# Down and output projections of a two-layer encoder trunk: activations stationary, weights streamed 512 columns at a time, sums turned back by TensorE

## The chip, the cores and the metric

The kernel runs on one NeuronCore of a Trainium2 chip. The metric is the device time of one execution in microseconds (us); the figure of a kernel is the median of its runs.

## The reference

The program computes two layers on 256 tokens of 1024 values, batch 1, in float32. Each layer is a SwiGLU feed-forward block (1024 to 2816 to 1024) in half step, a token mixer (retention, stick-breaking attention and a Mamba-2 SSD mixer beside each other, then one output projection from 1536 to 1024), and a second SwiGLU block. Every sub-layer is normalised and modulated ahead, and its result is gated into the residual `h`:

```python
for l in range(DEPTH):
    mod = (cond @ ada_w[l] + ada_b[l]).reshape(B, 3 * N_SUB, D_MODEL)[:, None]
    u = modulate(rmsnorm(h, norm_ffn1[l]), mod[:, :, 0], mod[:, :, 1])
    h = h + 0.5 * (1.0 + mod[:, :, 2]) * swiglu(u, ffn1_wg[l], ffn1_wu[l], ffn1_wd[l])
    u = modulate(rmsnorm(h, norm_mix[l]), mod[:, :, 3], mod[:, :, 4])
    proj = u @ w_in[l]
    ...
    mixed = jnp.concatenate([y_ret, y_sb, y_ssm], axis=-1) @ w_out[l]
    h = h + (1.0 + mod[:, :, 5]) * mixed
    u = modulate(rmsnorm(h, norm_ffn2[l]), mod[:, :, 6], mod[:, :, 7])
    h = h + 0.5 * (1.0 + mod[:, :, 8]) * swiglu(u, ffn2_wg[l], ffn2_wu[l], ffn2_wd[l])
return modulate(rmsnorm(h, final_norm), fmod[:, :, 0], fmod[:, :, 1])
```

The change concerns the last product of each sub-layer: `@ wd` of the four feed-forward blocks and `@ w_out` of the two mixers.

## The kernel before

**Layout.** Everything is held channel-major: `h`, the normalised input and all activations have channels on the 128 partitions and the 256 tokens along the free axis. A matmul takes 128 x 128 weights as the stationary operand and streams 256 tokens past it. `h` is one tile of eight column groups (1024 = 8 x 128), each 128 x 256.

**Precision.** Each float32 operand is split in two float32r parts, `hi` (ScalarE copies the value, L306) and `lo` (VectorE subtracts, L307). A product takes three matmuls: hi x hi, hi x lo and lo x hi (`mm3`).

**Weights.** They come in units of 128 x 2048 (two halves of 1024) through SyncE's DMA queue in a fixed order, are split half by half in `step`, and are asked for some halves ahead by `need` and `half`. `stream_order` also lays in the units of the modulation's weights, which VectorE multiplies (L266).

**A feed-forward block.** For each of eleven groups of 256 hidden channels, TensorE makes gate and up (`pg`, `pu`, 48 matmuls each), ScalarE and VectorE form the gated activation `g` (hi and lo), and one unit of the down projection (`out_unit`) adds its product to four PSUM banks `dn` (128 x 512, two column groups of `h` each). The mixer's output projection runs the same `out_unit` six times per layer into banks `wo`. A unit is 8 column groups x 2 halves x 3 = 48 matmuls of 256 columns. There are 44 units of down projections and 12 of output projections.

**The last unit of a sub-layer** goes bank by bank: as soon as bank b is complete, VectorE updates two column groups of `h` (L520), ScalarE makes the high part `hgh` of gain x h (two, L410) and the squares (L413, `norm_a`), and VectorE the low part `hgl` (two, L421) and the running sum of squares (L425, `norm_b`), while TensorE goes on with the next bank.

**The lead** (`lead`) opens the next sub-layer before its norm is known: for k = 0 to 5 it streams `hgh` and `hgl` of column group k past two weight units (`ld`, 12 matmuls of 258 columns each), at k = 5 it first sums the squares over the channels (`nps`), then VectorE and ScalarE make the inverse root (`diag`), TensorE spreads it, and the last two column groups follow. There are five leads; the last sub-layer ends in the final norm (`mean`, `fin`) instead.

**Order.** The program is one list written by hand (`manual_schedule`), and each engine runs its part of it in that order. PSUM has eight banks: four in a ring (`ring`) for projections, four for the accumulators (`accp`: four banks, or two pairs in the mixer), opened and closed per stage. `k4` is a pool of ten tiles of 4 KB a partition for activations.

Of the kernel before, what the change touches and what calls it, by code (L numbers as in the profile page):

```python
# [9 lines left out]
AF = mybir.ActivationFunctionType  # L10
ALU = mybir.AluOpType
PSUM = bass.MemoryType.PSUM

P = 128
# [43 lines left out]
ONES, IDENT, LATER, HIDDEN = range(4)  # L58
# [17 lines left out]
def downs(j, g0):  # L76
    done = 0
    for i in range(g0, j + 1):
        lo = done
        done = i if i - lo <= 2 else lo + 2  # L80
    return range(lo, done)
# [74 lines left out]
class Trunk:  # L156
# [292 lines left out]
        self.nc.vector.scalar_tensor_tensor(out=self.ul[:, c], in0=t, scalar=self.mods[:, self.shift + c:self.shift + c + 1],  # L449
                                            in1=self.uh[:, c].bitcast(F32), op0=ALU.add, op1=ALU.subtract)  # L450

    def lead(self, n, ends):
        nc = self.nc
        banks = [self.bank("ld") for _ in range(4)]

        def go(k, f):
            hf = k // 4
            hi, lo = self.w[n + f // 2, hf]
            cs = slice((f % 2) * P, (f % 2) * P + P)
            gh, gl = self.hg[hf]  # L460
            self.mm3(banks[f][:, 0:258], [hi[:, k % 4, cs], lo[:, k % 4, cs]], (gh[:, k % 4], gl[:, k % 4]), k == 0)

        self.need(n + 1, 1, 2)
        for k in range(6):
            if k == 5:
                self.norm_sum(self.acc("nps"))
                self.need(n + 1, 1, 3)
                self.norm_rstd()
                self.need(n + 1, 1, 4)
            for f in range(4):  # L470
                go(k, f)
        self.norm_bcast()
        bias = self.sm.tile([P, 4], F32, tag="lbias", name="lbias")
        ts, us = [], []
        for f in range(4):
            for k in (6, 7):
                go(k, f)
            nc.scalar.activation(out=bias[:, f:f + 1], in_=banks[f][:, 256:257], func=AF.Copy)
            us.append(self.apply_a(f))
            if f % 2 == 0:  # L480
                t = self.tk2("lt")
            ts.append(t[:, (f % 2) * 256:(f % 2) * 256 + 256])
            nc.vector.tensor_tensor(out=ts[f], in0=banks[f][:, 0:256], in1=self.rs, op=ALU.mult)
            if f:
                self.apply_b(f - 1, us[f - 1])
        for it in ((n, 0), (n + 1, 0), (n, 1), (n + 1, 1)):
            del self.w[it]
        for c in range(4, KD):
            us.append(self.apply_a(c))
            self.apply_b(c - 1, us[c - 1])  # L490
        self.apply_b(KD - 1, us[KD - 1])
        for f in range(4):
            ends(f, ts[f], bias[:, f:f + 1])
# [3 lines left out]

    def out_unit(self, accs, n, mov, first, last, gate):
        nc = self.nc
        dst = lambda d: accs[d // 2][:, (d % 2) * 256:(d % 2) * 256 + 256]  # L500

        def block(w, d, f):
            st = first and f == 0 and d % 2 == 0
            self.mm3(dst(d), [w[0][:, d * P:(d + 1) * P], w[1][:, d * P:(d + 1) * P]], mov[f], st)

        if not last:
            for f in range(2):
                w = self.half(n, f)
                for d in range(8):
                    block(w, d, f)  # L510
                    if d % 2:
                        self.tick()
            return
        ws = [self.half(n, 0, 7), self.half(n, 1, 6)]
        for b in range(4):
            for d in (2 * b, 2 * b + 1):
                for f in range(2):
                    block(ws[f], d, f)
            for d in (2 * b, 2 * b + 1):
                nc.vector.scalar_tensor_tensor(out=self.h[:, d], in0=dst(d), scalar=gate[:, d:d + 1], in1=self.h[:, d],  # L520
                                               op0=ALU.mult, op1=ALU.add)
            if self.hg is None and b == 2:
                nc.scalar.preload_act_table_set(SET_SQRT)
            self.norm_a(b)
            if b == 2 or self.hg and b:
                self.norm_b(b - 1)
        if self.hg:
            self.norm_b(3)

    def gate(self, col, half):  # L530
        g = self.sm.tile([P, 8], F32, tag="gate", name="gate")
        src = self.mods[:, col:col + 8]
        if half:
            self.nc.vector.tensor_scalar(out=g, in0=src, scalar1=1.0, scalar2=0.5, op0=ALU.add, op1=ALU.mult)
        else:
            self.nc.vector.tensor_scalar(out=g, in0=src, scalar1=1.0, scalar2=None, op0=ALU.add)
        return g
# [25 lines left out]

    def ffn(self, w0, gate_col, prep, start=None):
        nc = self.nc
        self.open_acc(False)
        n = w0 + 2
        pend = []

        def gated(sg):  # L570
            g = self.tk4("g", FR)
            gh, gl = (g[:, 2 * i:2 * i + 2] for i in range(2))
            flat = lambda t: t.rearrange("p a b -> p (a b)")
            self.split(flat(gh), flat(gl), sg)
            pend.append([(gh[:, f], gl[:, f]) for f in range(2)])

        def ends(f, t, b):
            v = sg[:, (f % 2) * 256:(f % 2) * 256 + 256]
            if f < 2:
                self.silu(out=v, in_=t, bias=b)  # L580
            else:
                nc.vector.scalar_tensor_tensor(out=v, in0=t, scalar=b, in1=v, op0=ALU.add, op1=ALU.mult)

        g0 = 1
        if start:
            g0 = GS
            banks = start()
            n = w0 + 2 * GS
            self.need(n, 0, 2)
            for j in range(GS):  # L590
                sg = self.tk2("sg")
                self.silu(out=sg, in_=banks[2 * j])
                nc.vector.tensor_tensor(out=sg, in0=sg, in1=banks[2 * j + 1], op=ALU.mult)
                gated(sg)
        else:
            sg = self.tk2("sg")
            self.lead(w0, ends)
            gated(sg)
        accs = None
        for j in range(g0, NJ):  # L600
            pg, pu = self.bank("pg"), self.bank("pu")
            pair = j == 1
            if pair:
                self.proj2(n, (pg, False, None), (pu, False, None))
            else:
                self.proj(pg, n)
            sg = self.tk2("sg")
            self.silu(out=sg, in_=pg)
            if not pair:
                self.proj(pu, n + 1)  # L610
            nc.vector.tensor_tensor(out=sg, in0=sg, in1=pu, op=ALU.mult)
            gated(sg)
            if j == g0:
                accs = [self.acc("dn") for _ in range(4)]
            n += 2
            for i in downs(j, g0):
                self.out_unit(accs, n, pend.pop(0), i == 0, False, None)
                n += 1
            if start and j == 7:
                nc.sync.dma_start(out=self.consts, in_=self.io["consts"])  # L620
                nc.sync.dma_start(out=self.wdt, in_=self.io["wdt"])
        gate = self.gate(gate_col, True)
        prep()
        self.out_unit(accs, n, pend.pop(0), False, True, gate)
        self.close_acc()

    def mix(self, l, w0, gate_col, prep):
        nc = self.nc
        st = {}
        flat = lambda t: t.rearrange("p a b -> p (a b)")  # L630
        V = lambda t, n: flat(t).rearrange("p (a b) -> p a b", a=n)
        self.open_acc(True)
        dt = self.sm.tile([P, 2, 8], F32, tag="dt", name="dt")
        dta = self.sm.tile([P, 2, 8], F32, tag="dta", name="dta")
        sc = float(P) ** -0.5
# [279 lines left out]
        def target(name):  # L915
            if name[:2] in ("sv", "rv"):
                return None, True, [self.bank("pv")[:, 0:264 if name == "sv0" else 256] for _ in range(2)]
            return self.bank("pj"), False, None
# [4 lines left out]
            self.silu(out=st["z"][:, f], in_=t, bias=b)  # L923

        begin = {3: [values()], 8: [stick(0)], 9: [stick(1)], 11: [ssm(0)], 12: [ssm(1)], 13: [state_scores()], 15: [ssm(2), ssm(3), retain(0)], 18: [retain(1)]}
        self.lead(w0, ends)
        n = w0 + 2
        for idx, name in enumerate(MIX_UNITS):
            if idx < 2:
# [2 lines left out]
            if idx == 2:  # L932
                ts = [target(name), target(MIX_UNITS[3])]
                self.proj2(n, *ts)
                done = [evac(name, ts[0]), evac(MIX_UNITS[3], ts[1])]
            elif idx > 3:
                t = target(name)
# [11 lines left out]
        accs = [self.acc("wo") for _ in range(4)]  # L949
        gate = self.gate(gate_col, False)  # L950
        for o, kk in enumerate(W_OUT_ORDER):
            hi, lo = st["mix", kk // 2]
            mov = [(hi[:, (2 * kk + f) % 4], lo[:, (2 * kk + f) % 4]) for f in range(2)]
# [2 lines left out]
                prep()  # L956
            self.out_unit(accs, n, mov, o == 0, o == 5, gate)
            n += 1
        self.close_acc()

    def run(self):
        nc = self.nc
# [132 lines left out]
```

## Time and profile before

| what | value |
|---|---|
| median of 3 runs | 1162.9 us (1162.77 to 1163.27) |
| span of the profiled execution | 1161.9 us |
| TensorE busy | 1126.8 us (97%), 9316 matmuls |
| VectorE busy | 893.3 us (77%) |
| ScalarE busy | 619.0 us (53%) |
| DMA | 282.63 MB, mean 243 GB/s |
| granted TensorE clock | 0.998 |

The profile is of one execution; its span runs from the first to the last instruction, and the median of the runs is 1.0 us longer. A row of the timeline gives the start (us from the span's start), the duration, the engine, the line of the kernel, the operation, output tile <- input tiles, the shape and how many were merged; in brackets the idle time of the engine ahead of it and what ended it. Rows of TensorE are matmuls (PE) and weight loads (PEld). Matmuls overlap, so a row's duration is longer than the step from one start to the next. A matmul in full float32 shows as two records, one in float32r as one.

### The profile page before, as it was taken

The page shows a single profiled execution, that of the slowest core. Times are in us where ns is not written, and L with a number is a line of the kernel's source. Part 1 is how long each engine was busy: PE and PEld are TensorE (multiplying, and loading weights), DVE is VectorE, ACT ScalarE, POOL GpSimd, SP SyncE. Part 2 cuts the span into 40 slices and gives each one's busy share as a digit, 9 for nine tenths or more (in the row PEclk, how much of TensorE's full clock was granted, in tenths as well). Part 3 has the DMA queues.
Part 4 walks back from the last instruction along what each step waited for, and adds up shares of the span by engine and source line. Part 5 has one row for each costly group of instructions (what it writes and reads, how often), then busy time and mean ns, then how long its engine had stood idle before and what let it go on. Part 6 is the DMA issues. An engine that isn't in the chain of part 4 may idle for free.

```text
span 1161.9 us, 22045 instructions
## 1 busy us (share of the span) xinstructions
PE 1126.8 (97%) x9316; PEld 1115.7 (96%) x9316; DVE 893.3 (77%) x1300; ACT 619.0 (53%) x870; POOL 0.2 (0%) x4
## 2 busy tenths in 40 slices
PE   1999999999999999999999999999999999999996
PEld 1999999999999999999999999999999999999996
DVE  6988786788778788898488788667886877977544
ACT  4464434586874464444466444457687546544432
POOL 0000000000000000000000000000000000000000
PEclk9999999999999999999999999999999999999999
DMA  9879898357454539999536988643655452987610
GB/s 376 338 265 366 320 361 333 129 214 276 163 190 155 182 142 370 347 372 359 188 110 258 345 322 307 254 182 144 256 182 186 177 189 80 351 331 283 235 58 37
DMA packets 39555, 282.63 MB, mean 243 GB/s; under 512 B 4384, under 2 KB 4640, under 8 KB 5408
## 3 DMA queue, kind: packets, MB, share of 16 engines
q1 hardware_dynamic: 39456, 281.22, 64.6%
q8 instruction: 73, 1.20, 0.4%
q14 instruction: 26, 0.21, 0.1%
HBM read 280.15 MB, written 1.05 MB: 242 GB/s over the span
## 4 chain that ended last, share of the span: by engine, by line
PE 96%; DVE 2%; ACT 1%; DMA 1%; issue 0%; SPq 0%; ACTq 0%; DVEq 0%
PE dn L198 21%; PE pu L198 19%; PE pg L198 19%; PE pj L198 14%; PE ld L198 7%; PE wo L198 6%; PE pv L198 4%; DVE raw_a L266 1%; PE seg L198 1%; PE nps L198 1%; DMA h<-in_x 1%; PE tail L198 1%; PE sz L198 1%; PE rn L198 1%; PE yb L198 1%; PE rs L198 0%
## 5 line engine op out<-in xcount | busy, mean ns | idle before, releaser
L307 DVE TENSOR_TENSOR lo<-raw_w,hi 128x1024 fp32r<-128x1024 f32 x368 | 441.6, 1222 | 152.8 <-ACT hi L306 152.5
L306 ACT ACTIVATE hi<-raw_w 128x1024 fp32r<-128x1024 f32 x368 | 380.3, 1053 | 252.4 <-DMA raw_w<-in_w 118.1
L198 PE MATMUL dn<-g,hi 128*128 128x256 f32 x1408 | 250.7, 280 | 0.0
L198 PEld LDWEIGHTS dn<-g,hi 128*128 128x128 f32 x1408 | 215.7, 189 | 0.0
L266 DVE CUSTOM_DVE_ANT_0 raw_a<-raw_a,cond,params 128x1024 f32<-128x1024 f32 x160 | 198.8, 1280 | 0.3 <-DMA raw_a<-in_ada 0.3
L198 PE MATMUL dn<-g,lo 128*128 128x256 f32 x704 | 197.3, 280 | 0.0
L198 PE MATMUL pu<-uh,hi 128*128 128x256 f32 x608 | 171.2, 282 | 0.0
L198 PE MATMUL pu<-ul,hi 128*128 128x256 f32 x608 | 171.2, 282 | 0.0
L198 PE MATMUL pg<-ul,hi 128*128 128x256 f32 x608 | 171.1, 281 | 0.0
L198 PE MATMUL pg<-uh,hi 128*128 128x256 f32 x608 | 171.1, 281 | 0.0
L198 PE MATMUL pg<-uh,lo 128*128 128x256 f32 x608 | 170.9, 281 | 0.0
L198 PE MATMUL pu<-uh,lo 128*128 128x256 f32 x608 | 170.8, 281 | 0.0
L198 PEld LDWEIGHTS dn<-g,lo 128*128 128x128 f32 x704 | 132.8, 189 | 0.0
L198 PE MATMUL pj<-uh,hi 128*128 128x256 f32 x448 | 127.9, 285 | 0.0
L198 PE MATMUL pj<-ul,hi 128*128 128x256 f32 x448 | 126.0, 281 | 0.0
L198 PE MATMUL pj<-uh,lo 128*128 128x256 f32 x448 | 125.9, 281 | 0.0
L198 PEld LDWEIGHTS pu<-uh,lo 128*128 128x128 f32 x608 | 114.9, 189 | 0.0
L198 PEld LDWEIGHTS pg<-uh,lo 128*128 128x128 f32 x608 | 114.8, 189 | 0.0
L198 PEld LDWEIGHTS pu<-ul,hi 128*128 128x128 f32 x608 | 114.5, 188 | 0.0
L198 PEld LDWEIGHTS pg<-ul,hi 128*128 128x128 f32 x608 | 114.4, 188 | 0.0
L198 PEld LDWEIGHTS pg<-uh,hi 128*128 128x128 f32 x608 | 114.4, 188 | 0.0
L198 PEld LDWEIGHTS pu<-uh,hi 128*128 128x128 f32 x608 | 114.3, 188 | 0.0
(189 smaller groups left out, 1791.2 us busy)
## 6 DMA issues: line engine op xcount, KB each, us to landing
raw_w<-in_w SPq DMA_DIRECT2D x184, 1024.0 KB, 5.8
raw_a<-in_ada SPq DMA_DIRECT2D x80, 1024.0 KB, 6.5
consts<-in_consts SPq DMA_DIRECT2D x1, 1216.0 KB, 10.1
h<-in_x SPq DMA_DIRECT2D x1, 1024.0 KB, 7.0
out<-fin SPq DMA_DIRECT2D x4, 256.0 KB, 2.3
cond<-in_c SPq DMA_DIRECT2D x1, 512.0 KB, 4.3
mats<-in_mats SPq DMA_DIRECT2D x1, 256.0 KB, 7.1
params<-in_params SPq DMA_DIRECT2D x1, 176.0 KB, 4.4
```

Of the source, the lines that this page charges most:

```text
L198: self.nc.tensor.matmul(out, lhsT=lhsT, rhs=rhs, start=start, stop=True, skip_group_check=True)
L266: nc.vector.tensor_tensor_reduce(out=raw[:, f * 1024:(f + 1) * 1024], in0=raw[:, f * 1024:(f + 1) * 1024], in1=self.cond, scale=1.0, scala ...
L306: self.nc.scalar.activation(out=hi, in_=src, func=AF.Copy)
L307: self.nc.vector.tensor_tensor(out=lo, in0=src, in1=hi.bitcast(F32), op=ALU.subtract)
```

## The change

**The units.** The two operands change places. The activations (128 channels x 128 tokens, hi or lo) are the stationary operand and the weights stream past, 512 columns at a time, so the sums come out token-major: bank 2 dh + tb holds 128 tokens (tb) x 512 channels (dh). A unit is 24 matmuls of 512 columns. The weights' order and their splits are the same.

**The last unit of a sub-layer** goes through its four banks one after the other. ScalarE copies each complete bank into SBUF (`y`, two tiles from `k4`), and TensorE turns it back with eight transposes of 128 x 128 per half of the channels (`turn`, into two banks `yt` that are taken from the same four). VectorE then updates `h` from `yt`. The first half is turned after the third bank's matmuls; the second half is turned in `tail`, which the next `lead` calls after its first 12 matmuls. `tail` also closes the accumulators' pool, and the pool of the next stage is opened right after it. Without a next lead (end of the program) `tail` runs at once. At that end the squares are also summed on VectorE, so that the `mean` takes two matmuls and not six.

```diff
     def lead(self, n, pairs, ends):
...
             for f in range(4):
                 go(k, f)
+            if k == 0:
+                self.tail()
+                self.open_acc(pairs)
...
-        dst = lambda d: accs[d // 2][:, (d % 2) * 256:(d % 2) * 256 + 256]
-
-        def block(w, d, f):
-            st = first and f == 0 and d % 2 == 0
-            self.mm3(dst(d), [w[0][:, d * P:(d + 1) * P], w[1][:, d * P:(d + 1) * P]], mov[f], st)
+        def block(w, f, dh, tb):
+            ts, ds = slice(tb * P, tb * P + P), slice(dh * 512, dh * 512 + 512)
+            for i, (a, b) in enumerate(((0, 0), (0, 1), (1, 0))):
+                self.mm(accs[2 * dh + tb], mov[f][a][:, ts], w[b][:, ds], first and f == 0 and i == 0)
 
         if not last:
             for f in range(2):
                 w = self.half(n, f)
-                for d in range(8):
-                    block(w, d, f)
-                    if d % 2:
+                for dh in range(2):
+                    for tb in range(2):
+                        block(w, f, dh, tb)
                         self.tick()
             return
         ws = [self.half(n, 0, 7), self.half(n, 1, 6)]
-        for b in range(4):
-            for d in (2 * b, 2 * b + 1):
-                for f in range(2):
-                    block(ws[f], d, f)
-            for d in (2 * b, 2 * b + 1):
-                nc.vector.scalar_tensor_tensor(out=self.h[:, d], in0=dst(d), scalar=gate[:, d:d + 1], in1=self.h[:, d],
-                                               op0=ALU.mult, op1=ALU.add)
+        ys = [self.tk4("y") for _ in range(2)]
+
+        def copy(dh, tb):
+            nc.scalar.activation(out=ys[dh][:, 2 * tb:2 * tb + 2].rearrange("p a b -> p (a b)"), in_=accs[2 * dh + tb], func=AF.Copy)
+
+        def turn(dh):
+            ts = [self.acc("yt") for _ in range(2)]
+            y = ys[dh].rearrange("p a b -> p (a b)")
+            for tb in range(2):
+                for i in range(4):
+                    nc.tensor.transpose(ts[i // 2][:, (i % 2) * 256 + tb * P:(i % 2) * 256 + tb * P + P],
+                                        y[:, tb * 512 + i * P:tb * 512 + i * P + P], self.mat(IDENT))
+            return ts
+
+        def update(b, t):
+            for f in range(2):
+                d = 2 * b + f
+                nc.vector.scalar_tensor_tensor(out=self.h[:, d], in0=t[:, f * 256:(f + 1) * 256], scalar=gate[:, d:d + 1],
+                                               in1=self.h[:, d], op0=ALU.mult, op1=ALU.add)
             if self.hg is None and b == 2:
                 nc.scalar.preload_act_table_set(SET_SQRT)
             self.norm_a(b)
-            if b == 2 or self.hg and b:
-                self.norm_b(b - 1)
-        if self.hg:
+
+        for i in range(4):
+            dh, tb = divmod(i, 2)
+            for f in range(2):
+                block(ws[f], f, dh, tb)
+            if i < 3:
+                copy(dh, tb)
+            if i == 2:
+                ts = turn(0)
+        update(0, ts[0])
+        copy(1, 1)
+        update(1, ts[1])
+        self.norm_b(0)
+
+        def tail():
+            ts = turn(1)
+            update(2, ts[0])
+            self.norm_b(1)
+            update(3, ts[1])
+            self.norm_b(2)
             self.norm_b(3)
+            self.close_acc()
+
+        self.tail = tail
+        if self.hg is None:
+            tail()
```

In `ffn` and `mix` the calls that opened and closed the accumulators' pool at the ends of a stage fall away.

On TensorE, at the first change of stage (last unit of the first down projection, then the lead of the mixer), these rows stand before; `hi`, `lo` are weight halves:

```order
L198 MATMUL dn<-g,hi_0_2072 128x256 x2
L198 MATMUL dn<-g,lo_0_2073 128x256
L198 MATMUL dn<-g,hi_1_2102 128x256 x2
L198 MATMUL dn<-g,lo_1_2103 128x256
L198 MATMUL ld<-hgh,hi_0_2132 128x258
L198 MATMUL ld<-hgl,hi_0_2132 128x258
L198 MATMUL ld<-hgh,lo_0_2133 128x258
```

and these now, where `yt` are the transposes:

```order
L198 MATMUL dn<-hi_1_1886,g 128x512
L528 MATMUL yt<-mats,y 128x128 x8
L198 MATMUL dn<-hi_0_1868,g 128x512
L198 MATMUL dn<-lo_0_1869,g 128x512
L198 MATMUL dn<-hi_0_1868,g 128x512
L198 MATMUL dn<-hi_1_1886,g 128x512
L198 MATMUL dn<-lo_1_1887,g 128x512
L198 MATMUL dn<-hi_1_1886,g 128x512
L198 MATMUL ld<-hgh,hi_0_1916 128x258
L198 MATMUL ld<-hgl,hi_0_1916 128x258
```

The first eight transposes stand ahead of the last bank's six matmuls, and the second eight (not in these rows) after twelve `ld` matmuls.

On ScalarE at the same place, before:

```order
L306 ACTIVATE hi_0_2294<-wdt 128x4x8
L410 ACTIVATE hgh<-h,gs 128x256 x2
L413 ACTIVATE sq<-h 128x512
L410 ACTIVATE hgh<-h,gs 128x256 x2
L413 ACTIVATE sq<-h 128x512
```

and now:

```order
L306 ACTIVATE hi_0_2054<-wdt 128x4x8
L521 ACTIVATE y<-dn 128x512 x3
L410 ACTIVATE hgh<-h,gs 128x256 x2
L413 ACTIVATE sq<-h 128x512
L521 ACTIVATE y<-dn 128x512
L410 ACTIVATE hgh<-h,gs 128x256 x2
```

Three copies stand ahead of the first `hgh`, and the fourth behind the first square.

On VectorE at the end of the program, before:

```order
L347 SCALAR_TENSOR_TENSOR gs<-mods,params 128x8
L520 SCALAR_TENSOR_TENSOR h<-dn,gate,h 128x256 x6
L425 TENSOR_TENSOR sq<-sq 128x512
L520 SCALAR_TENSOR_TENSOR h<-dn,gate,h 128x256 x2
L983 TENSOR_SCALAR fin<-h,gs 128x256 x8
L984 RECIPROCAL rs<-rs 128x256
```

and now:

```order
L347 SCALAR_TENSOR_TENSOR gs<-mods,params 128x8
L535 SCALAR_TENSOR_TENSOR h<-yt,gate,h 128x256 x6
L425 TENSOR_TENSOR sq<-sq 128x512
L535 SCALAR_TENSOR_TENSOR h<-yt,gate,h 128x256 x2
L425 TENSOR_TENSOR sq<-sq 128x512 x2
L1017 TENSOR_SCALAR fin<-h,gs 128x256 x8
L1018 RECIPROCAL rs<-rs 128x256
```

Two sums of squares have come in ahead of the eight `fin`; the updates read `yt` and not `dn`.

More of the change, by code (lines that the diff above doesn't have):

```diff
@@ L450, in apply_b, with lead @@
                                             in1=self.uh[:, c].bitcast(F32), op0=ALU.add, op1=ALU.subtract)
-    def lead(self, n, ends):
+    def lead(self, n, pairs, ends):
         nc = self.nc
@@ L565, in ffn @@
         nc = self.nc
-        self.open_acc(False)
         n = w0 + 2
@@ L586, in ffn @@
             g0 = GS
+            self.open_acc(False)
             banks = start()
@@ L596, in ffn @@
             sg = self.tk2("sg")
-            self.lead(w0, ends)
+            self.lead(w0, False, ends)
             gated(sg)
@@ L624, in ffn @@
         self.out_unit(accs, n, pend.pop(0), False, True, gate)
-        self.close_acc()
     def mix(self, l, w0, gate_col, prep):
@@ L631, in mix @@
         V = lambda t, n: flat(t).rearrange("p (a b) -> p a b", a=n)
-        self.open_acc(True)
         dt = self.sm.tile([P, 2, 8], F32, tag="dt", name="dt")
@@ L925, in mix @@
         begin = {3: [values()], 8: [stick(0)], 9: [stick(1)], 11: [ssm(0)], 12: [ssm(1)], 13: [state_scores()], 15: [ssm(2), ssm(3), retain(0)], 18: [retain(1)]}
-        self.lead(w0, ends)
+        self.lead(w0, True, ends)
         n = w0 + 2
@@ L958, in mix @@
             n += 1
-        self.close_acc()
     def run(self):
```

## The prediction

> **What bounds the kernel now.** I read the page first (busy times, then the chain that ended last), then the costliest groups, then the timeline of TensorE around one down projection, one attention burst and one change of stage, and last the timelines of VectorE and ScalarE there.
>
> ```profile
> span 1161.9 us, 22045 instructions
> PE 1126.8 (97%) x9316; PEld 1115.7 (96%) x9316; DVE 893.3 (77%) x1300; ACT 619.0 (53%) x870; POOL 0.2 (0%) x4
> PE 96%; DVE 2%; ACT 1%; DMA 1%; issue 0%; SPq 0%; ACTq 0%; DVEq 0%
> L198 PE MATMUL dn<-g,hi 128*128 128x256 f32 x1408 | 250.7, 280 | 0.0
> L198 PE MATMUL dn<-g,lo 128*128 128x256 f32 x704 | 197.3, 280 | 0.0
> ```
>
> TensorE is 97% busy and is 96% of the chain, and the matmuls of the down projections (1408 + 704) have no idle time ahead of them. So a microsecond taken from or given to TensorE's queue moves the end by a microsecond. What counts is the step from the start of one matmul to the start of the next, not the 280 ns that each shows, because they overlap. The two windows below are two of the 56 units (44 of down projections, 12 of output projections) of 48 matmuls each; behind the length of the window stand the busy time of TensorE, of its weight loads and of VectorE on this tile, then the granted clock.
>
> ```profile
> 441.13:446.76 5.63, 5.63 (x48) 5.59 (x48) 0.00 (x0) 1.00 0.96 389
> 458.18:463.89 5.71, 5.71 (x48) 5.67 (x48) 0.00 (x0) 1.00 1.02 418
> ```
>
> A unit takes 5.67 us at the full granted clock (1.00), so a step of 256 columns is 5.67 / 48 = 0.118 us.
>
> **The change, part by part.** (a) *Half as many matmuls, twice as wide.* A unit becomes 24 matmuls of 512 columns; the columns streamed are the same, so only what a matmul costs beside its columns can be saved. No float32r matmul of 512 columns stands in the trace. The nearest are 384 wide, in a burst of the SSD mixer (4 of 384 and 4 of 128 columns, between matmuls of 256):
>
> ```profile
> 299.25 0.28 PE L198 MATMUL pj<-uh,lo 128*128 128x256 f32 x1
> 299.37 1.25 PE L198 MATMUL seg<-segm,mats 128*128 128x384 f32 x8
> 300.46 0.33 PE L198 MATMUL pj<-uh,hi 128*128 128x256 f32 x1
> 300.63 0.29 PE L198 MATMUL pj<-ul,hi 128*128 128x256 f32 x1
> 300.75 0.28 PE L198 MATMUL pj<-uh,lo 128*128 128x256 f32 x1
> 372.77 0.86 PEld L198 LDWEIGHTS rn<-mats,rsq 128*128 128x128 f32 x7 [0.24 <-issue]
> 371.92 1.02 PE L198 MATMUL rn<-diag,mats 128*128 128x512 f32 x2
> 372.77 0.95 PE L198 MATMUL rn<-mats,rsq 128*128 128x1 f32 x8
> ```
>
> From 299.25 to 300.75 there are 1.50 us: three matmuls of 256 (0.35) and the burst, so a pair of 384 + 128 takes 1.15 / 4 = 0.287. The 128-wide one cannot be shorter than a weight load. Loads that wait for nothing else follow each other every (0.86 - 0.19) / 6 = 0.112 us (0.19 is what one of these loads shows). That leaves 0.175 for 384 columns. From 256 to 384 the step thus grows by 0.057, so for 512 columns I extrapolate 0.118 + 2 x 0.056 = 0.230 us. The steps grow almost with the columns: the time seems to lie in the stream, not in the load.
> Bounds: in proportion to the columns 0.236 (gain nothing); the other end is the row of 512 columns in full float32, one matmul of the code that shows as two records, which last until the next start 372.77 - 371.92 = 0.85, hence 0.425 for 512 columns, about half the rate of the float32r steps. If float32r at 512 took half of that and a little for the change of weights, its step would be 0.215. I take 0.230 because the 384-wide row is of the same data type. Gain: 2 x 0.118 - 0.230 = 0.006 per pair, with 1344 pairs 7.8 us (0 to 28).
>
> The Trainium skill ("TensorE: Matmul & The Clock Gate", section "Back-to-back issue gap") gives N / 2.4 + 2.5 ns, an estimate of 216 ns for 512 columns and 109 for 256. The trace disagrees at 256: 118. By that rule alone the gain would be 1344 x (236 - 216) = 27 us.
>
> (b) *96 transposes, 16 in each of the six last units.* The same form stands in the trace, eight in a row:
>
> ```profile
> 274.70 0.28 PE L198 MATMUL pj<-uh,lo 128*128 128x256 f32 x1
> 274.81 1.03 PE L711 MATMUL xt<-mats,xs 128*128 128x128 f32 x8
> 275.60 0.36 PE L198 MATMUL pj<-uh,hi 128*128 128x256 f32 x1
> 275.81 0.28 PE L198 MATMUL pj<-ul,hi 128*128 128x256 f32 x1
> ```
>
> From 274.70 to 275.81 there are 1.11 us, less two matmuls of 256 (0.236): 0.87 us for eight, 0.109 each. In all 96 x 0.109 = 10.5 us on TensorE, with nothing that hides them. They alone cost more than (a) brings.
> The same page of the Trainium skill (section "Part 4: PE-mode transpose") speaks harder against the change: about 275 ns per transpose inside a kernel. No run here shows it; by that figure, as an estimate, the 96 would be 26 us.
>
> (c) *The wait at the next stage's first matmul.* Before, VectorE updates two column groups of h while TensorE goes on with the next two, and the normalised input of the next stage is ready early. The rows of the first change of stage:
>
> ```profile
> 218.67 0.28 PE L198 MATMUL ld<-hgh,hi 128*128 128x258 f32 x1
> 219.99 0.87 DVE L520 SCALAR_TENSOR_TENSOR h<-dn,gate,h 128x256 f32<-128x256 f32 x2
> 220.78 0.87 DVE L421 SCALAR_TENSOR_TENSOR hgl<-h,gs,hgh 128x256 fp32r<-128x256 f32 x2
> 222.96 0.68 DVE L425 TENSOR_TENSOR sq<-sq 128x512 f32<-128x512 f32 x1
> 220.50 0.91 ACT L410 ACTIVATE hgh<-h,gs 128x256 fp32r<-128x256 f32 x2 [0.46 <-DVE h L520]
> 221.32 0.62 ACT L413 ACTIVATE sq<-h 128x512 f32<-128x512 f32 x1
> 372.97 0.60 ACT L882 ACTIVATE rr<-rn 128x512 f32<-128x512 f32 x1 [0.63 <-PE rn L198]
> 225.84 0.95 PE L198 MATMUL nps<-mats,sq 128*128 128x1 f32 x8
> 228.48 0.70 PE L198 MATMUL nps<-diag,mats 128*128 128x256 f32 x2 [0.16 <-DVE diag L341]
> ```
>
> I count from the start of the last unit (213.0 = 218.67 - 5.67). A block is six matmuls, 1.38 us. Three blocks end at 4.14, the first eight transposes at 5.01, the fourth block at 6.39. The first two output banks' copies (0.60 each, as the rr row) end before 4.14. The sixth transpose fills the first turned bank at about 5.06 (a transpose shows 0.27 us). VectorE then has two pairs of updates (0.87 each, 0.79 apart): 5.06 to 6.8, and only then the low part hgl of column group 0: ready at 7.3. TensorE wants it for the second `ld` matmul at 6.5. Stall: 0.8 us, five times. Queued behind the waiting matmul is all of the next stage; VectorE and ScalarE wait for nothing there that it holds.
> ScalarE's fourth copy stands behind the hgh pair and the square (0.91 + 0.62 from 5.5) and ends at 7.6. That is before TensorE asks for it at 8.6 (7.3 and eleven more `ld` matmuls of 0.12), so this copy and the other three are hidden by TensorE's work; with that cover gone each would cost 0.6.
>
> (d) *The second turn, inside the lead.* It runs from 8.6 to 9.5. VectorE then has update, hgl pair, sum of squares, update, hgl pair, sum, hgl pair, sum, in which the update pair takes 0.79, the hgl pair 0.79 and the sum 0.6 from start to start. From 9.5 that is 0.8 x 5 + 0.6 x 3 = 5.8, so the last sum ends at about 15.3 to 15.5. TensorE does four groups of 12 matmuls (5.8 us) and asks for it at 15.2: a stall of 0.2. Before it came at 222.96 + 0.68 = 223.64 and was asked for at 225.84, a slack of 2.2 us which the change uses up. The next wait, for the diagonal (0.16), stays as it is, since its chain starts from the nps matmuls.
> A change of stage thus costs 16 x 0.109 + 0.8 + 0.2 = 2.75, say 2.8 us; five make 14.0. Bounds: no stall at all, 1.75 each; or VectorE one weight split later (1.2 us) at both waits, 4.5 each.
>
> (e) *The end of the program.* Here the tail is not covered by a lead.
>
> ```profile
> 1148.97 0.68 DVE L425 TENSOR_TENSOR sq<-sq 128x512 f32<-128x512 f32 x1
> 1149.60 0.88 DVE L520 SCALAR_TENSOR_TENSOR h<-dn,gate,h 128x256 f32<-128x256 f32 x2
> 1150.39 2.18 DVE L983 TENSOR_SCALAR fin<-h,gs 128x256 f32<-128x256 f32 x8
> 1153.17 1.75 DVE L984 RECIPROCAL rs<-rs 128x256 f32<-128x256 f32 x1 [0.60 <-ACT rs L980]
> 1149.80 2.83 PE L198 MATMUL mean<-sq,mats 128*128 128x256 f32 x12 [0.24 <-DVE sq L425]
> ```
>
> Counted from the last unit's start (1143.8), the reciprocal starts at 9.4 now. After the change the fourth block ends at 6.4, its copy at 7.4 and the second turn at 8.4. VectorE goes on with update (to 9.3), sum (9.9), update (10.8), two sums (12.1) and the eight `fin` (2.18): 14.3. The mean's matmuls, two in place of six (four rows of twelve), end ahead of that, so the sums on VectorE, not TensorE, are late next. The end moves by 4.9 to 5.0 us, both turns included (3.5 to 6.5).
>
> (f) Costed at nothing: 24 copies of 0.60 on ScalarE (53% busy; covered but for what (c) and (e) count), two more buffers of the ten in the k4 pool (those they take were last read before the last unit), and the weights' transfers and splits, which keep their number and order.
>
> **The sum.** -7.8 + 14.0 + 5.0 = +11.2 us. The profiled execution's span is 1161.9, 1.0 under the median of the runs, 1162.9; on the median the forecast is 1174.
>
> **Rivals.**
> 1. *The load was the bound (faster).* If a step of 256 columns is set by its weight load and the stream runs free at 512, the step is 0.215: 1162.9 - 28 + 19 = 1154. For it: the load's cadence of 0.112 is close to 0.118, and the full-float32 rows show no excess. Against it: 384 columns took 0.175, where columns at the same rate would take 0.161 to 0.163. It decides for faster from a step under 0.220 (gain 21.3 = 19 + 2.3); between 0.220 and 0.223 it is no change. Chance 0.14 for the first, 0.06 for the second. The rule of the skill's section on the issue gap would end here: by its 216 ns, 1155.
> 2. *The stream is the bound.* 0.236 a step, nothing saved: 1162.9 + 19 = 1182. For it: 0.118 per 256 and 0.175 per 384 are nearly in proportion. Chance 0.2.
> 3. *The stalls hide.* VectorE reaches hgl in time and only the transposes and the end stay: 1162.9 - 7.8 + 8.7 + 5.0 = 1169. Chance 0.15.
> 4. *Transposes are dearer than in the burst,* because the two turns stand between other stages of the array: at 0.272, what one shows alone, 96 x 0.163 = 15.6 more, 1190. Against it: the burst's 0.109 stood between the same kind of matmuls. Chance 0.03. The figure of 275 ns on the skill's page would land here too.
> The forecast itself has 0.42.
>
> **How the numbers follow.** 1174 is the likeliest case; its own range is 1168 to 1180, from steps of 0.228 to 0.234 and stalls between none and twice mine. The range of 8 in 10 reaches to the other cases of slower and halfway into the faster one: 1158 to 1184. Within 0.2% (2.3 us) is about what a measurement cannot tell from no change. Faster has 0.14, from rival 1; no change 0.06; slower 0.80, from the forecast and rivals 2 to 4.
>
> **What would show it.** In the profile after: a unit of 24 matmuls takes 5.5 us (5.2 would be rival 1, 5.67 rival 2); `yt` groups of eight take 0.87; the second `ld` matmul waits 0.8 us for VectorE's hgl at each of five changes of stage, the `nps` sum waits 0.2; the reciprocal starts 14.3 us after the last unit's start. A step far under 0.23, or waits where a buffer or a weight comes late that I counted as covered, would make the forecast wrong.

## The result and the profile after

The changed kernel takes 1177.4 us (median; 1176.3 to 1178.4), beside 1163.1 for the kernel before on the same chip: ratio 1.0125, 95% interval 1.0111 to 1.0139. It is slower by 14.3 us; the forecast was 1174, +11.2.

The page of the changed kernel, the lines that answer to those of before (span, busy times by engine, the chain's shares, the two groups of the down projections):

```profile
span 1175.3 us, 19515 instructions
PE 1134.5 (97%) x8060; PEld 1060.6 (90%) x8060; DVE 895.1 (76%) x1302; ACT 634.2 (54%) x894; POOL 0.2 (0%) x4
PE 95%; DVE 3%; ACT 1%; DMA 1%; issue 0%; SPq 0%; ACTq 0%; DVEq 0%
L198 PE MATMUL dn<-hi,g 128*128 128x512 f32 x704 | 227.8, 395 | 0.0
L198 PE MATMUL dn<-lo,g 128*128 128x512 f32 x352 | 138.7, 394 | 0.0
```

TensorE shows 1256 records fewer (7870 matmuls in place of 9122) and is still the chain: 95%. Two units of down projections of the changed kernel, in windows for the tile `dn` (length; busy time of TensorE, its loads and ScalarE on the tile; granted clock; DMA share; GB/s):

```profile
427.27:432.83 5.56, 5.56 (x24) 4.33 (x24) 0.00 (x0) 1.00 0.55 192
444.25:449.87 5.62, 5.61 (x24) 4.34 (x24) 0.00 (x0) 1.00 1.00 391
```

24 wide matmuls take 5.56 to 5.62 us, where 48 took 5.63 to 5.71. The loads now leave TensorE's load path idle for a fifth of the unit (4.33 of 5.56), and it buys little. The first change of stage, TensorE's timeline:

```profile
215.51 1.03 PE L528 MATMUL yt<-mats,y 128*128 128x128 f32 x8
216.30 0.48 PE L198 MATMUL dn<-hi,g 128*128 128x512 f32 x1
...
217.77 0.28 PE L198 MATMUL ld<-hgh,hi 128*128 128x258 f32 x1
218.47 0.39 PE L198 MATMUL ld<-hgl,hi 128*128 128x258 f32 x1 [0.43 <-DVE hgl L421]
...
219.90 1.04 PE L528 MATMUL yt<-mats,y 128*128 128x128 f32 x8
220.69 0.37 PE L198 MATMUL ld<-hgh,hi 128*128 128x258 f32 x1
220.90 0.28 PE L198 MATMUL ld<-hgl,hi 128*128 128x258 f32 x1
...
226.43 0.28 PE L198 MATMUL ld<-hgh,lo 128*128 128x258 f32 x1
226.74 1.02 PE L198 MATMUL nps<-mats,sq 128*128 128x1 f32 x8
```

Each turn of eight holds TensorE for 0.79 us (215.51 to 216.30, 219.90 to 220.69), and the matmul behind it has a step 0.09 longer. The second `ld` matmul starts 0.70 after the first, where a step is 0.12: 0.58 lost, put down to VectorE's `hgl`. The `nps` sum starts 0.31 after the last `ld` matmul: 0.19 lost (0.19 to 0.23 at the five changes of stage). VectorE there:

```profile
216.37 1.66 DVE L535 SCALAR_TENSOR_TENSOR h<-yt,gate,h 128x256 f32<-128x256 f32 x4 [2.35 <-PE yt L528]
217.94 0.87 DVE L421 SCALAR_TENSOR_TENSOR hgl<-h,gs,hgh 128x256 fp32r<-128x256 f32 x2
```

Four updates stand ahead of the low part that TensorE waits for; VectorE itself had been idle for 2.35 us, waiting for the turn. The end of the program, in the timeline:

```profile
1159.50 0.66 PE L528 MATMUL yt<-mats,y 128*128 128x128 f32 x4 [0.25 <-ACT y L521]
1163.75 2.08 PE L198 MATMUL mean<-sq,mats 128*128 128x256 f32 x4 [3.59 <-DVE sq L425]
1163.61 2.19 DVE L1017 TENSOR_SCALAR fin<-h,gs 128x256 f32<-128x256 f32 x8
1166.37 1.75 DVE L1018 RECIPROCAL rs<-rs 128x256 f32<-128x256 f32 x1 [0.57 <-ACT rs L1014]
```

The last unit starts at 1152.17, so the reciprocal starts 14.2 us behind it. Before, the last unit started at 1143.71 and the reciprocal 9.5 us behind it.

### The profile page after: what moved, and what is told of

Its sections match the earlier page's. It is cut to its first block, busy times and chain, and to the rows that moved or that the text cites. A ratio compares the mean times of both kernels' runs of the same rounds, so it can differ in the third digit from the quotient of the medians.

```text
span 1175.3 us, 19515 instructions
## 1 busy us (share of the span) xinstructions
PE 1134.5 (97%) x8060; PEld 1060.6 (90%) x8060; DVE 895.1 (76%) x1302; ACT 634.2 (54%) x894; POOL 0.2 (0%) x4
## 4 chain that ended last, share of the span: by engine, by line
PE 95%; DVE 3%; ACT 1%; DMA 1%; issue 0%; SPq 0%; ACTq 0%; DVEq 0%
PE dn L198 21%; PE pu L198 18%; PE pg L198 18%; PE pj L198 14%; PE ld L198 7%; PE wo L198 5%; PE pv L198 4%; DVE h L535 1%; DVE raw_a L266 1%; PE yt L528 1%; PE seg L198 1%; PE nps L198 1%; PE tail L198 1%; PE sz L198 1%; PE rn L198 1%; DMA h<-in_x 1%
## 5 line engine op out<-in xcount | busy, mean ns | idle before, releaser
L198 PE MATMUL dn<-hi,g 128*128 128x512 f32 x704 | 227.8, 395 | 0.0
L198 PEld LDWEIGHTS dn<-hi,g 128*128 128x128 f32 x704 | 132.2, 188 | 29.3
L198 PE MATMUL dn<-lo,g 128*128 128x512 f32 x352 | 138.7, 394 | 0.0
L198 PEld LDWEIGHTS pu<-uh,lo 128*128 128x128 f32 x608 | 114.9, 189 | 0.0
L198 PEld LDWEIGHTS pj<-uh,hi 128*128 128x128 f32 x448 | 84.3, 188 | 0.7 <-issue 0.7
```

The lines of the kernel that those rows point to most:

```text
L198: self.nc.tensor.matmul(out, lhsT=lhsT, rhs=rhs, start=start, stop=True, skip_group_check=True)
```

## The experiments

All share the kernel before on their chip (1162.8 to 1163.0 in the runs below). Theory: the wide step saves a few us, the turns and the waits behind them cost more, and nothing else moves.

**1. The wide matmuls alone.** The kernel before with the new matmuls. It leaves out the turning back: the sums stay token-major and go into `h` as they are.

```diff
-            self.mm3(dst(d), [w[0][:, d * P:(d + 1) * P], w[1][:, d * P:(d + 1) * P]], mov[f], st)
...
+            for i, (x, y) in enumerate(((0, 0), (0, 1), (1, 0))):
+                for c in range(0, 512, 512):
+                    self.mm(accs[b][:, c:c + 512], mov[f][x][:, ts], w[y][:, dh * 512 + c:dh * 512 + c + 512], first and f == 0 and i == 0 and c == 0)
```

> The kernel before with the wide matmuls alone: activations stationary, 512 columns of weights streamed, 24 matmuls a unit. No copies and no transposes: the updates of h read the token-major sums as they are (the part left out is the turning back; the amount of work behind it is the same). Theory (a wide matmul costs its stream, 0.2325 us against twice 0.118): each of the 56 units saves 0.083 us, so 1163.1 - 4.7 = 1158.4, and the rest of the 14 us of the change is the turning. Rival (the wide matmuls bring nothing, or are held up by weights that come late): 1163. Rival (the load was the bound and the turning hid the gain): 1163.1 - 1344 x 0.020 = 1136.

Measured: 1158.8 us (1158.4 to 1159.2), ratio 0.9967 [0.9954, 0.9980]. The wide step is worth 4.1 us as the buffers lie here, no more. A unit in a window that counts all of TensorE's rows (24 and neighbours at the edges):

```profile
422.39:428.00 5.61, 5.61 (x27) 4.51 (x26) 4.65 (x6) 3.83 (x6) 0.00 (x0) 1.00 0.55 187
```

**2. The roles swapped, at 256 columns.** As 1, with two matmuls of 256 columns for each wide one.

> As the run of the wide matmuls without turning, but 256 columns at a time: the operands have changed places and a unit is 48 matmuls as before; the same loads are made twice. Nothing is turned back here either. Theory (only the number of matmuls counts, not which operand streams): 1163.1, within 1.5. Rival (streamed weights are dearer than streamed activations, and the wide step of 0.2325 is a large saving of loads less this price): 2688 x 0.015 = 40 more at full saving, anything from 1168 to 1203.

Measured: 1163.7 us, ratio 1.0007 [0.9998, 1.0017]. Swapping the operands costs nothing that shows here; the gain of 1 is the width.

**3. The low part ahead of the second update.** One line of the changed kernel moved:

```diff
         copy(1, 1)
+        self.norm_b(0)
         update(1, ts[1])
-        self.norm_b(0)
```

> The changed kernel with the low part of the first column groups (norm_b(0)) made ahead of the second pair of updates on VectorE. Theory (the second ld matmul waits 0.43 to 0.58 us for that low part and for nothing else at five changes of stage): 1177.4 - 5 x 0.55 = 1174.6, and the gap ahead of that matmul is under 0.1. Rival (VectorE's chain as a whole is late, the wait moves to the sum of squares): 1177.4, the wait ahead of nps grows by what the first one shrinks.

Measured: 1175.4 us, ratio to before 1.0104 [1.0087, 1.0121]: 2.0 less than the change as made, 2.8 expected. VectorE now makes `hgl` behind two updates:

```profile
217.26 0.88 DVE L535 SCALAR_TENSOR_TENSOR h<-yt,gate,h 128x256 f32<-128x256 f32 x2 [2.35 <-PE yt L528]
218.32 0.89 DVE L421 SCALAR_TENSOR_TENSOR hgl<-h,gs,hgh 128x256 fp32r<-128x256 f32 x2 [0.19 <-ACT hgh L410]
```

The wait at the second `ld` matmul is gone in all five changes of stage; the steps of all `ld` matmuls together fall from 103.2 to 101.0 us. The order of VectorE's list was the cause of that wait. The `nps` wait stays, as it is set by the second turn.

**4. Every turn twice.** 192 transposes in place of 96; the second set writes the same values again.

```diff
-            for tb in range(2):
+            for tb in (0, 1, 0, 1):
```

> The changed kernel with every transpose made twice, 192 in place of 96, into the same places. Theory (a transpose costs its 0.109 us in full on TensorE): 1177.4 + 96 x 0.109 = 1187.9. Rival (TensorE waits for VectorE or ScalarE behind the turns anyway, so that a part is hidden): 1180 to 1184. Rival (a transpose beside other work costs more than its place in the row of eight): over 1191.

Measured: 1186.8 us, ratio 1.0208 [1.0193, 1.0224]: 9.4 more than the change. From the start of a turn to the next other matmul, all turns take 24.28 us in place of 13.80: 96 more cost 10.48 on TensorE, 0.109 each, as forecast. The time shows 1.1 us less than that. In the profile 0.7 came back at the end: here the `mean` matmuls took 1.13 us, not 2.08, and their steps sum to 0.75 in place of 1.44 (see 6). The rest is within the spread of the executions (1186.4 to 1188.1 here).

TensorE's timeline of this run, a first turn and the end:

```profile
215.72 1.91 PE L528 MATMUL yt<-mats,y 128*128 128x128 f32 x16
217.38 0.48 PE L198 MATMUL dn<-hi,g 128*128 128x512 f32 x1
...
1174.42 1.13 PE L198 MATMUL mean<-sq,mats 128*128 128x256 f32 x4 [3.59 <-DVE sq L425]
```

The turn of sixteen holds TensorE for 1.66 us, that of eight for 0.79.

**5. The second turn at once.** In the changed kernel `tail()` runs ahead of the lead rather than behind its first column group.

```diff
     def lead(self, n, pairs, ends):
         nc = self.nc
+        self.open_acc(pairs)
...
-            if k == 0:
-                self.tail()
-                self.open_acc(pairs)
...
-        if self.hg is None:
-            tail()
+        tail()
```

> The changed kernel with the second turn and what follows it (tail) right behind the fourth bank at all six ends, not inside the next lead. Theory (the twelve ld matmuls ahead of the second turn cover the fourth copy and the updates): without that cover TensorE waits about 0.8 us for the copy, and the lead's low part, now behind four updates or made before them as in the program, is ready by then; so about 0.3 to 0.8 more at each of five changes of stage, 1179 to 1181. Rival (the cover is worth nothing because the lead waits for VectorE there anyway): 1177.4 or up to 2 less.

Measured: 1175.7 us, ratio 1.0110 [1.0095, 1.0125]: 1.7 less. My theory gave the turn's place inside the lead a worth; this fell. TensorE's timeline and one row of VectorE's:

```profile
218.13 0.60 PE L526 MATMUL yt<-mats,y 128*128 128x128 f32 x4
219.21 0.66 PE L526 MATMUL yt<-mats,y 128*128 128x128 f32 x4 [0.48 <-ACT y L519]
219.62 0.37 PE L198 MATMUL ld<-hgh,hi 128*128 128x258 f32 x1
219.82 0.28 PE L198 MATMUL ld<-hgl,hi 128*128 128x258 f32 x1
224.84 0.68 DVE L425 TENSOR_TENSOR sq<-sq 128x512 f32<-128x512 f32 x1
226.88 0.95 PE L198 MATMUL nps<-mats,sq 128*128 128x1 f32 x8
```

The uncovered copy costs one wait of 0.48 between the two halves of the turn. While TensorE waits and turns, VectorE gets its low parts done: no wait at the second `ld` matmul (0.20 behind the first, the long step that follows any turn), and the last sum is done at 225.52, 1.4 us ahead of `nps`. One wait replaces two.

**6. TensorE kept busy at the end.** 28 matmuls on constants (`dm`) between the last turn and `mean`, in the changed kernel.

> The changed kernel with 28 added matmuls of 256 columns of a constant (their result is read by nobody) behind the last turn, where TensorE otherwise sits idle for 3.6 us ahead of the mean. Theory (the idle stretch makes the granted clock fall to a half, so that the mean's four rows take 2.08 us and not 0.9, and the reciprocal waits 0.57 for them): the clock stays at 1.00, the mean takes about 0.9, the reciprocal starts behind the eight fin with no wait, end 0.5 to 0.6 earlier in the profile. Rival (the four rows are slow for another reason, such as the first matmuls after a wait): they take 2.08 again.

Measured, in one execution: 1177.05 us. The timeline:

```profile
1160.51 3.59 PE L198 MATMUL dm<-mats 128*128 128x256 f32 x28
1164.34 1.13 PE L198 MATMUL mean<-sq,mats 128*128 128x256 f32 x4 [0.25 <-DVE sq L425]
1164.20 2.19 DVE L1021 TENSOR_SCALAR fin<-h,gs 128x256 f32<-128x256 f32 x8
1166.30 1.75 DVE L1022 RECIPROCAL rs<-rs 128x256 f32<-128x256 f32 x1
```

`mean` takes 1.13 us, not 2.08, and the reciprocal follows the eight `fin` without a wait: 2.10 behind their start, 2.76 in the changed kernel. In the changed kernel the clock fell while TensorE was idle ahead of `mean`, as windows over it show (granted clock behind POOL's busy time):

```profile
1140.00:1156.00 16.00, 16.00 (x98) 14.17 (x97) 1.53 (x4) 2.43 (x4) 0.00 (x0) 1.00 0.00 1
1159.50:1163.70 4.20, 0.66 (x4) 0.42 (x4) 3.56 (x8) 3.02 (x4) 0.00 (x0) 0.86 0.00 0
1163.70:1166.00 2.30, 2.08 (x4) 1.18 (x4) 2.10 (x8) 0.14 (x1) 0.00 (x0) 0.50 0.01 4
```

That fits the theory, but one execution does not prove that the dummies did it: in 4 (row above) and in 11 below TensorE is idle for the same 3.59 and 3.58 us ahead of `mean`, with no dummies, and the clock stays. The rows of 8 (clock 0.50) and of 11 (0.99):

```profile
1140.19 2.07 PE L198 MATMUL mean<-sq,mats 128*128 128x256 f32 x4 [3.59 <-DVE sq L427]
1165.34 1.13 PE L198 MATMUL mean<-sq,mats 128*128 128x256 f32 x4 [3.58 <-DVE sq L427]
```

Of the six profiled executions with this end and no dummies, four have the slow `mean` (the changed kernel, 3, 5 and 8) and two the fast one (4 and 11). An idle stretch of this length halves the clock in some executions and not in others. This is worth 0.6 us at the end and no more.

**7. and 8. Where the streamed operand starts.** Wide steps came out unequal, 0.228 to 0.234. Joining each matmul's two start addresses in the compiled program with its step in the trace, I found that steps of one shape differ by address. So the normalised input (`uh`, `ul`), streamed by the gate, up and mixer projections, was moved by 96 bytes, from 128 to 224 modulo 256: in 7 in the kernel before, in 8 in the changed kernel. Two scratch tiles have one buffer to make room.

```diff
+        self.pad0 = self.cp.tile([P, 24], F32, name="pad0")
         self.uh = self.cp.tile([P, KD, S], FR, name="uh")
         self.ul = self.cp.tile([P, KD, S], FR, name="ul")
+        self.pad1 = self.cp.tile([P, 8], F32, name="pad1")
...
```

> The kernel before with the normalised input (uh, ul) 96 bytes further in each partition, so that it starts at 224 in place of 128 within 256 bytes; nothing else is changed but two small scratch buffers that are single (for the room) and what lies between shifted by 128 bytes. Theory (the excess of a float32r step over its columns depends on how the addresses of the streamed and of the loaded operand stand to each other; in the rows of before, streams that start at 96 or 224 took 0.1147 to 0.1176 and those at 128 took 0.1182 to 0.1198): the steps of pg, pu and pj fall from 0.119 to about 0.116, 4992 x 0.003 = 15 us, 1148. Rival (the differences belong to the tiles and stages, not to addresses): 1163.

> The changed kernel with the same shift of the normalised input. Theory (addresses): the same 15 us less than the changed kernel, 1162, and the ratio to the kernel before with the shift is that of the two without it. Rival: 1177.

Measured: 7 takes 1138.0 us, ratio 0.9785 [0.9768, 0.9801], 10 us less than expected; 8 takes 1153.4, ratio 0.9919 [0.9904, 0.9933], 24 less than the change as made and 9 less than expected. The change thus costs as much with the input moved: 1153.4 / 1138.0 = 1.0136. Some 96 steps of the gate and up projections in windows, of the kernel before and then of 7 (the counts in brackets take in neighbours at the edges):

```profile
429.69:441.13 11.44, 11.44 (x98) 11.44 (x97) 11.44 (x15) 4.18 (x5) 0.00 (x0) 1.00 0.93 357
```

```profile
454.03:464.93 10.90, 10.90 (x99) 10.90 (x97) 8.91 (x13) 4.66 (x5) 0.00 (x0) 1.00 0.90 337
```

119.2 ns a step became 113.5, at the same granted clock.

**9. to 11. Is it the stream's own start?** 9 and 10 are 7 with pads that put the input at 0 and at 192; 11 is 8 with the weights' parts moved by 64 bytes as well.

> The kernel before with the lead's normalized input (uh, ul) moved by 128 bytes, so that its rows start at 0 modulo 256; every other buffer stands where it stood in the run with the input at 224, and the two scratch tiles have one buffer as there. Theory, the step depends on where the streamed operand starts: streams that started at 0 or 128 took 118.0 to 119.8 ns in the run before, so nothing is gained: 1160 to 1165 us. Rival, it was the shift of the other buffers or the scratch tiles: 1138 us as in that run.

> As the run with the input at 0, but with the input's rows at 192 modulo 256. Theory: down projections whose streams started at 64 or 192 took 117.0 to 118.4 ns a step, some 1.3 ns less than at 128, in some 5000 steps: about 1157 us (1153 to 1162). Rival, any start that is not a multiple of 128 is as good as 224: 1138 us.

> The changed kernel with the input at 224 modulo 256, and the weights' high and low parts moved by 64 bytes, so that the 512 streamed columns start at 96 or 224 instead of 32 or 160. Theory, the stream's start decides in wide steps too: the 256-column step lost 3.5 ns at such starts, so a wide one loses 3.5 to 7 ns from 232.7, in 1056 steps: 3.7 to 7.4 us less than the 1153.4 us of the changed kernel with the input alone moved, 1146 to 1150 us. Rival, a wide step doesn't depend on it: 1153 us.

Measured: 9 takes 1162.95 us, ratio 1.0002 [0.9992, 1.0011]; moving things by itself does nothing. 10 takes 1154.8, ratio 0.9928 [0.9912, 0.9945]. Both as the theory had it. But 11 takes 1178.2, ratio 1.0133 [1.0117, 1.0148]: 25 us worse than 8, where 4 to 7 less were expected. Its input still stood at 224, and the window shows 119.3 ns again:

```profile
433.75:445.20 11.45, 11.45 (x98) 11.44 (x96) 11.45 (x15) 4.25 (x5) 0.00 (x0) 1.00 0.94 344
```

So the stream's own start is not what decides, and that theory fell. I sorted the steps anew, by the start of the streamed operand less the start of the next matmul's stationary operand. So sorted, all runs agree but for the row 64 (mean step in ns, worked out from all float32r steps of 256 columns in the traces):

| difference | before | 7 | 9 | 10 | 11 |
|---|---|---|---|---|---|
| 256 columns, 0 modulo 128 | 119.0 | 119.0 | 119.1 | 119.2 | 119.3 |
| 32 | 117.7 | 117.6 | 117.6 | 117.4 | - |
| 64 | 116.0 | 114.6 | 116.1 | 115.9 | - |
| 96 | 119.0 | 118.7 | 119.1 | 118.9 | - |

In the kernel before, the 4948 steps of the projections stand at 96; in 7 at 64, in 10 at 32, in 11 nearly all at 0. The row 64 is lower in 7 because 6072 steps stand in it there, most of them of gate and up (`pg` 114.9, `pu` 113.5). In the kernel before it holds 612 steps, of down and output projections (115.4 to 118.0), so the difference is not all that sets a step. In nearly all of these steps (8126 of 8154 before) the matmul's own stationary operand gives the same difference as the next one, so the runs do not tell which of the two counts.

**12. The weights moved, the input not.** The kernel before with the weights' parts moved by 32 bytes, which also makes the difference 64.

```diff
+        self.pad1 = self.cp.tile([P, 8], F32, name="pad1")
         self.rs = self.cp.tile([P, S], F32, name="rs")
...
```

> The kernel before with only the weights' high and low parts moved, by 32 bytes, to 64 or 192 modulo 256 (a small scratch tile has one buffer to make room); the input stays where it was, at 128. Joined with the addresses, the traces so far order the 256-column steps by one number, the start of the streamed operand minus the start of the next stationary operand, modulo 128: 64 gives 114.6 ns, 32 gives 117.4, 0 and 96 give 119.0, in every run alike. New theory, this difference decides: 4948 steps of the projections go from 96 to 64, as they did in the run with the input at 224, so about 1138 us (1135 to 1142). Rival, the streamed operand's own start decides: the input hasn't moved, 1161 to 1164 us.

Measured: 1138.5 us, ratio 0.9792 [0.9776, 0.9809], and 113.6 ns a step:

```profile
470.37:481.28 10.91, 10.91 (x98) 10.91 (x97) 8.81 (x11) 7.04 (x8) 0.00 (x0) 1.00 0.87 332
```

The difference of the two starts sets the gain, whichever operand is moved. 7 and 12 beat both kernels of this case.

## Why the prediction came out as it did

The sign and the mechanism were right: the bound stayed TensorE's queue, and what was put into it came out at the end. The sum was 3.1 us short, from terms that were mis-sized, in the prediction's own order. Sums of steps are taken from one start to the next on TensorE, over the whole profiled execution.

- **(a) The wide step**, 0.230 forecast, gain 7.8. Measured 0.2327 in the mean of the `dn` steps that nothing delays; all `dn` steps together went from 249.3 to 245.7 us and all `wo` steps from 69.9 to 68.9, a gain of 4.65 (4.1 in experiment 1). This is the term that failed, by 3.2 us: as much as the whole miss. I extrapolated along columns from one burst of the mixer. The starts inside that burst do not split as I assumed: the next start comes 0.173 us behind the first 384-wide matmul, 0.227 behind the other three, and 0.06 behind the 128-wide ones. So neither the floor of 0.112 for the narrow ones nor the 0.175 that it left for 384 columns stands in the trace, and 0.230 came as near as it did partly by luck. In the changed kernel steps with a difference of 0 or 64 modulo 256 do take about 230 (229.7 to 230.1), but they are a quarter (315 of 1268 steps from one wide matmul to the next); the others take 232.4 to 234.0. Rival 1, a step of 0.215 or 0.220 set by the load, is refuted: with the loads idle a fifth of the time the step still follows the columns. Rival 2, the stream as the bound (0.236, 1182 us), was nearer the truth than its chance of 0.2 said, though 1 shows that a gain was there.
The Trainium skill ("TensorE: Matmul & The Clock Gate", section "Back-to-back issue gap") gives N / 2.4 + 2.5 ns for the isolated gap at the full clock, an estimate of 216 ns for 512 columns; the trace disagrees, with 232.7.
- **(b) The transposes**, 0.109 each, 10.5 us: measured 0.79 from a turn's start to the next matmul and 0.09 in the step behind it, 0.88 where 0.87 was forecast; experiment 4 gives 10.48 for 96. Rival 4 is out: its 0.272 is how long the row of one transpose lasts (0.273 in the mean of the 96 here), and the rows overlap.
- **(c) The wait for the low part**, 0.8: measured 0.58. The cause was right (experiment 3). Counted from the last unit's start (215.51 - 18 x 0.233 = 211.32), the matmul that waits starts at 7.15, where I had the low part ready at 7.3, and TensorE was ready for it at 6.57 rather than 6.5. Two sums on the way were off and did no harm: the sixth transpose ends at 4.14 + 5 x 0.109 + 0.27 = 4.96 and not at 5.06 (the first update started at 5.05), and one weight split later at both waits makes 2.75 + 2 x 1.2 = 5.15 and not 4.5 (2.7 was measured). TensorE's waits over the whole execution name it (us in total, times, longest):

```profile
PE ld L198 <- DVE hgl L421: 2.1, 5, 0.4
```

- **(d) The second turn**: the wait at `nps` was 0.19 to 0.23 where 0.2 was forecast. The next wait, for the diagonal, did not stay as it was: 0.21 to 0.23 us in place of 0.14 to 0.16. And 5 shows that the place of the turn, which I had taken as cover, saved nothing: it is 1.7 us cheaper ahead of the lead. Over five changes of stage, the turns (2 x 0.79), the `ld` steps (98.1 to 103.2) and the `nps` steps (20.9 to 21.3) sum to 7.9 + 5.1 + 0.4 = 13.4, beside 14.0 forecast.
- **(e) The end**, 4.9 to 5.0: measured 4.7, reciprocal at 14.2 us behind the last unit's start against 14.3. It came out near by two misses that cancel: the eight `fin` ended 0.65 earlier than counted (1163.61 + 2.19 is 13.65 behind the unit's start, against 14.3), and the `mean` matmuls, said to be early, held the reciprocal up by 0.57 at half the clock.
- **(f)** The copies were hidden but for the last one of the program, which (e) counts (0.25 ahead of the second half of the last turn). No wait of TensorE for a weight is added.

Measured terms: -4.65 + 13.4 + 4.7 = 13.5 of 14.3. The span grew by 13.4, but it starts 0.75 us nearer to the first matmul than before (11.49 and 12.24 in the two traces); from the first matmul to the end of the span the growth is 14.2. Some 0.7 us of that is in none of the terms: 0.26 stand behind the reciprocal (8.95 to the end of the span in place of 8.69), and the rest is not traced.

Rival 3 (the waits hide, 1169) is refuted by its place: both waits stand in the trace. Experiments 3 and 5 show that reordering wins back 1.7 to 2.0 us of them, which does not change the sign.

## What to carry to other kernels

When TensorE's queue is the bound and its steps already follow the streamed columns, halving the number of matmuls may buy little (here 1.5% of those matmuls' time); price everything that the new layout puts into that queue (here 96 transposes) before it. When consumers of a turned result hang on one VectorE list, put what TensorE asks for first at the head of it, and don't count on cover without naming what waits meanwhile. Before changing the algorithm, look whether steps of one shape are equal; if they differ by operand, try an offset of 32 or 96 bytes for one of the two operands: here it cost no more than the second buffer of one or two scratch tiles and was worth five to six times the wide matmuls (24.4 to 24.8 us against 4.1 to 4.65). Moving the second operand as well (11) lost it all again.

## What the runs showed of the hardware that I had not expected

- A float32r matmul's step depends on where its streamed operand starts relative to the stationary operands (the next one's or its own, which the runs do not separate): at 256 columns 114.6 to 116 ns for a difference of 64 modulo 128, 117.5 for 32, 119.0 for 0 and 96; at 512 columns about 230 for 0 or 64 modulo 256, 232.4 to 234 else. The `ld` steps of 258 columns show no such order (119 to 122 at every difference). Moving either operand gives the same (1138.0 and 1138.5 us; 1162.95 and 1178.2 as the counter-tests). Why the difference counts, and why the wide steps follow 256, is open. The Trainium skill ("SBUF — State Buffer", section "Operand start alignment") speaks of where an operand may start and says that its runs timed nothing; these runs show that the start of one operand relative to the other has a price.
- 3.6 us without a matmul can halve the granted clock: four rows of `mean` took 2.08 us at 0.50 in the changed kernel, 1.13 in experiments 4 and 11 behind the same idle time. The Trainium skill ("TensorE: Matmul & The Clock Gate", section "Part 1: The HAM clock gate") gives an idle window of about 3.4 us that runs free of the kernel; both outcomes at 3.6 us agree with that, though no run here shows the window itself.
- Eight PE transposes of 128 x 128 in float32 between other matmuls cost 0.109 us each, in the burst of before, in the turns and doubled. The same page of the Trainium skill (section "Part 4: PE-mode transpose") has about 275 ns for one in bf16 inside a kernel, as a duration. The rows here last 0.273 us each, which agrees; but they overlap, and the queue pays 0.109.
